# Hybrid two-layer backbone: 512 weight columns per matmul in the products with stationary activations

## The chip, the cores and the metric

The kernel runs on one core of a Trainium2 chip. The metric is device time in microseconds of one execution. The kernel before takes 1544.28 us, the median of 3 runs (1542.03, 1544.28, 1546.81).

## What is computed

There are 256 latent tokens and 256 context tokens of width 2048, and two layers that share their weights between the two sets of tokens. All arithmetic is float32. Cut to what the change touches:

```python
# layer 0 (even): two branches side by side, one output projection
y = concatenate([za * silu(g_a), zb * silu(g_b)], -1) @ w_out      # 512 tokens, [2048, 2048]
# post-norm with a gate: t = ALPHA * x + gate * y; normed, scaled, shifted -> input of layer 1
# layer 1 (odd): grouped-query attention, 16 query heads, 4 key and value heads of 128
q, k, v, g = split(z @ w_in)                # k and v: 512 columns each, for latents and context
q, k = rms_norm(q), rms_norm(k)             # per head; rotary positions on the latents' q and k
o = softmax(q @ [k, k_ctx].T * 128 ** -0.5) @ [v, v_ctx]
y = (o * silu(g)) @ w_out                   # latents only: 256 tokens, [2048, 2048]
# again t = ALPHA * h + gate * y, and a layer norm over the 2048 columns gives the output
```

## The kernel before, in words

**Split products.** Each operand is kept as the sum of a high and a low part of type fp32r, and each product is three matmuls (high times high, high times low, low times high). Activations lie transposed in `big_h` and `big_l` (channels on the partitions, 16 tiles of 128 channels, 512 tokens: context first, then latents).

**The weight stream** (class `Stream`, from line 338). Weights come in pieces of 1024 words a partition (512 KB). A piece is loaded from SyncE's queue, ScalarE makes its high part (`high`: hi<-raw or hix<-raw), VectorE subtracts to get the low part (`low`: lo<-raw,hi or lox<-raw,hi). There are four buffers for raw pieces and four or more for each part; a buffer comes free when its last reader is through. `fill` (line 395) issues high and low parts as far ahead as there are buffers, `get` (line 415) calls `fill` and hands out the next piece. In the last projection `ws.more(wpool3, hi=3, lo=4)` (line 1852) makes the low buffers eight, and the `ws.fill()` behind it issues low parts up to eight pieces ahead at once.

**Two kinds of products.** `aform` has the weights stationary (128 output columns) and moves tokens. `bform` (line 497) has the activations stationary and moves the weights: 256 output columns, two token tiles side by side in the two halves of one PSUM bank. It is made of four `bpart`s (line 506), each of one weight piece of 4 k tiles by 256 columns and 24 matmuls of 128x256: 12 for the first token tile, `pump()`, 12 for the second, `pump()`. The banks of products come from `mbank`, a pool of two used in turn (line 265).

**Order of the work.** The program is unrolled in Python and its order is final: each engine executes what it was given in that order, and the first instruction that has to wait holds up all behind it on its engine. `Clock` and `Timed` estimate where each engine is while the program is written out. Generators that were handed to `background` (norms, key processing, attention heads, adaLN products) get their next step issued by `pump()` once that estimate says its inputs are ready; `force` issues the rest of one of them.

**Layer 0's output projection** (`layer0_half`, line 1566), once for the context, once for the latents: eight chunks of 256 columns. Each is one `bform`, then on VectorE, for both token tiles at once, `t = product * gate` (the read that frees the bank), `t = ALPHA * xp + t`, and two `bn_stats`. `xp` is loaded by GpSimd's queue. The first two context chunks are begun ahead, with the channels of the S5 branch first. `norm_h1` (line 1587) norms the whole half in the background, its 1/std on GpSimd, and turns it into `big_h`, `big_l` over PSUM banks of the pool `bb` (five banks here, line 1543).

**Keys and values of layer 1** (from line 1704), context then latents: four `bform`s, two for keys, two for values. Each of the key ones starts `k_done` (line 1682) in the background: step 1 copies the product (ScalarE `kn`), squares and sums it and computes 1/rms with twelve small GpSimd instructions (`rms`, line 1659); step 2 scales and rotates on VectorE; step 3 transposes on TensorE into a bank of `bb` and splits the result.

**Heads of layer 1** (line 1788): for each pair of heads one `bform` for queries, two `aform`s for gates, and attention in the background with banks of `bb`.

**The last projection** (from line 1808): chunks of 256 columns. Three quarters of each of the first two are begun among the last heads. After their last quarters ScalarE copies both into `t`, then comes `ws.fill()`, and then a loop over chunks 0 to 5: `load_h1(n + 1)` (GpSimd's queue; two buffers), the `bform` of the chunk (for n of 2 and more), `h1(n)` (two VectorE instructions `xp<-xp,gbr` that rebuild the layer's input), `t = product * gate1`, `t = ALPHA * xp + t`, `bn_stats`. The last two chunks run one token tile after the other, so that the norm of the first lies behind the products of the second. The norm's gain and shift `gf` are loaded by GpSimd's queue behind the last `load_h1` (lines 1866 and 1867).

Of the kernel before, what the change touches and what calls it, by code (L numbers as in the profile page):

```python
# [23 lines left out]
F32 = mybir.dt.float32  # L24
# [3 lines left out]
OP = mybir.AluOpType  # L28
# [4 lines left out]
T = 256            # latent tokens, and as many context tokens  # L33
NT = 512           # tokens in all: context first, then latents
# [19 lines left out]
class Clock:  # L54
    """Estimates of when each engine is through with what was issued to it, for the order of issue: engines run
    what they are given in order, an instruction waits for those that wrote what it reads and for those that
    read or wrote what it writes."""
# [72 lines left out]
    def dma(self, q, words, descr, outs, ins):  # L130
# [5 lines left out]
        while left > 0:                                       # room in buckets of 2 us  # L136
# [10 lines left out]
    def slot(self, pool, name, bufs, tile):  # L147
        """The tile takes the place of the one of that name bufs tiles ago."""
# [15 lines left out]
    def free(self, pool, name, bufs, n=1):  # L164
        """When n more tiles of that name have their places free."""
# [17 lines left out]
class Pool:  # L183
    """A pool whose tiles the clock knows."""
# [16 lines left out]
class Timed:  # L201
    """An engine whose instructions advance the clock."""
# [46 lines left out]
def backbone(ctx: ExitStack, tc: tile.TileContext, A, out):  # L249
# [15 lines left out]
    mm = pool(ctx, name="mm", bufs=2, space=bass.MemoryType.PSUM)  # L265
# [17 lines left out]
    def vacant():  # L283
        """Steps until the bank of hbank() is free."""
# [7 lines left out]
    def mbank():  # L292
        return mm.tile([P, 512], F32, name="m")
# [4 lines left out]
    # ---------------------------------------------------------------- constants  # L298
# [5 lines left out]
    negm = tabs[:, 0:64]                                     # window of the neighbourhood  # L304
# [3 lines left out]
    # small vectors as columns: 0 c, 16 c_ctx, 32 ln_g0, 48 ln_b0, 64 glu_b  # L308
# [11 lines left out]
    # silu of both conditioning vectors as stationary columns (32 wide, the rest zero)  # L320
# [10 lines left out]
    # sums over two sets of the vectors' shifts and scales  # L331
# [3 lines left out]
    mod = [const.tile([P, 2, 2, KT], F32, name=f"mod{l}") for l in range(2)]   # [shift|1+scale, c|c_ctx, kt], from the biases on  # L335

    # ---------------------------------------------------------------- streamed weights
    class Stream:
        """Pieces of weights, each at most PIECE words a partition, loaded and split ahead of their use."""
# [3 lines left out]
        def __init__(self):  # L343
# [3 lines left out]
            self.cap = CAP                            # pieces loaded ahead of use, at most  # L347
# [7 lines left out]
        def tile(self, kind, dtype):  # L355
            """In place of the oldest of its kind."""
# [38 lines left out]
        def fill(self):  # L395
            """Low and high parts as far ahead as there is room, and loads."""
# [13 lines left out]
        def ahead(self):  # L410
            """Loads, once there is room for them."""
# [3 lines left out]
        def get(self):  # L415
            """The next piece; those behind it are on their way."""
# [9 lines left out]
    # ---------------------------------------------------------------- background work  # L426
    bg = []                                                   # [generator, when its next step may be issued]
# [5 lines left out]
    def force(b, done=lambda: False):  # L433
        """Issue the steps of one of them up to a point that what follows builds on."""
# [1513 lines left out]
```

## Time and profile before

| what | us |
|---|---|
| median of the runs | 1544.28 |
| span of the profiled execution (the page gives no other time of it) | 1544.0 |
| TensorE busy | 1489.3 (96%) |
| VectorE busy | 983.3 (64%) |
| ScalarE busy | 642.2 (42%) |
| GpSimd busy | 153.5 (10%) |
| chain that ended last | TensorE 80%, VectorE 6%, DMA 5%, issue 4% |

A matmul's recorded duration is longer than its distance to the next one, because matmuls are pipelined; how fast TensorE works is read from the distances of their starts. A row of a timeline is: start, duration, engine, line, operation, output<-inputs, shapes, how many in a row are merged, and in brackets the idle time before it and what ended it. All instructions have the line of one helper (L212), so tiles tell them apart: `m<-hi,big_h` is a product of the weight stream, `b<-ident,...` a transpose.

### The profile page before, as it was taken

To read this page: it belongs to the slowest core of one execution; us is meant where nothing else is said; L and a number is where in the kernel's file an instruction comes from. 1 tells how busy PE (TensorE), PEld (TensorE's weight loads), DVE (VectorE), ACT (ScalarE), POOL (GpSimd) and SP (SyncE) were. 2 spreads that over 40 slices of the span, in tenths; PEclk is the share of its full clock that TensorE was granted. 3 is DMA by queue.
4 is the path that set the end of the run, shared out by engine and by line. 5 is a ranking of instruction groups with operands and counts; after the bars stand their busy time and mean duration, and the time that the engine had idled before them with its cause. 6 is when DMAs were issued, how large, how long until landed. Compare 5 with 4: busy or idle time off the path is not lost.

```text
span 1544.0 us, 30572 instructions
## 1 busy us (share of the span) xinstructions
PE 1489.3 (96%) x12530; PEld 1276.8 (83%) x12530; DVE 983.3 (64%) x1721; ACT 642.2 (42%) x981; POOL 153.5 (10%) x308
## 2 busy tenths in 40 slices
PE   6999988999999999999999999999999999999995
PEld 3676776677699977888887899999998888999995
DVE  5356489988522787545476564866764555677587
ACT  2332334422355434434353433543543445665540
POOL 1000000000000032300000000201321111121021
PEclk9999999999999999999999999999999999999998
DMA  9999365676888686543479998665658775445684
GB/s 327 338 320 305 115 187 185 202 238 219 256 294 260 175 201 153 150 142 110 128 229 316 308 314 259 190 196 167 219 183 269 246 232 178 137 124 151 204 255 141
DMA packets 329921, 332.71 MB, mean 215 GB/s; under 512 B 40197, under 2 KB 287925, under 8 KB 329141
## 3 DMA queue, kind: packets, MB, share of 16 engines
q1 hardware_dynamic: 323540, 314.87, 65.6%
q0 software_dynamic: 6240, 15.88, 3.9%
q8 instruction: 98, 1.61, 0.4%
q14 instruction: 43, 0.34, 0.1%
HBM read 301.92 MB, written 24.54 MB: 211 GB/s over the span
## 4 chain that ended last, share of the span: by engine, by line
PE 80%; DVE 6%; DMA 5%; issue 4%; POOL 2%; SPq 1%; ACT 1%; DVEq 0%; POOLq 0%; ACTq 0%
PE m L212 60%; PE b L212 10%; PE a L212 6%; PE sb L212 4%; DVE dd L212 2%; SPq L212 1%; DVE t L212 1%; DMA aw<-in_ada_w_dram 1%; DMA gf<-in_ln_b_dram 1%; DMA nat<-in_s_c_im_dram 1%; DVE lo L212 1%; DMA adp<-in_ada_w_dram 1%; POOL gbr L212 1%; POOL rt L212 1%; DMA xs<-in_x_dram 0%
## 5 line engine op out<-in xcount | busy, mean ns | idle before, releaser
L212 ACT ACTIVATE hi<-raw 128x1024 fp32r<-128x1024 f32 (+1 forms) x253 | 265.3, 1050 | 313.6 <-PE m L212 170.8
L212 PE MATMUL m<-hi,big_h 128*128 128x256 f32 x1224 | 352.9, 288 | 1.4 <-DVE t L212 1.4
L212 PE MATMUL m<-hi,big_l 128*128 128x256 f32 x1224 | 346.2, 283 | 0.0
L212 DVE TENSOR_TENSOR lo<-raw,hi 128x1024 fp32r<-128x1024 f32 (+1 forms) x214 | 257.3, 1209 | 110.4 <-issue 56.3
L212 PE MATMUL m<-lo,big_h 128*128 128x256 f32 x1152 | 325.7, 283 | 0.0
L212 PE MATMUL m<-big_h,hi 128*128 128x512 f32 (+1 forms) x848 | 321.4, 379 | 2.1 <-DVE acc L212 1.4
L212 PE MATMUL m<-big_l,hi 128*128 128x512 f32 (+1 forms) x848 | 309.0, 364 | 0.0
L212 PE MATMUL m<-big_h,lo 128*128 128x512 f32 (+1 forms) x832 | 304.4, 366 | 0.0
L212 PEld LDWEIGHTS m<-hi,big_h 128*128 128x128 f32 x1224 | 234.2, 191 | 17.3 <-issue 16.2
L212 PEld LDWEIGHTS m<-hi,big_l 128*128 128x128 f32 x1224 | 234.3, 191 | 0.2 <-DVE big_l L212 0.2
L212 PEld LDWEIGHTS m<-lo,big_h 128*128 128x128 f32 x1152 | 220.7, 192 | 0.2
L212 PEld LDWEIGHTS m<-big_h,hi 128*128 128x128 f32 x848 | 159.9, 189 | 47.7 <-issue 20.0
L212 PEld LDWEIGHTS m<-big_h,lo 128*128 128x128 f32 x832 | 156.9, 189 | 26.6
L212 PEld LDWEIGHTS m<-big_l,hi 128*128 128x128 f32 x848 | 160.3, 189 | 20.7
L212 PE MATMUL m<-lox,big_h 128*128 128x256 f32 x384 | 108.6, 283 | 0.0
L212 PE MATMUL m<-hix,big_h 128*128 128x256 f32 x312 | 89.3, 286 | 0.0
L212 PE MATMUL m<-hix,big_l 128*128 128x256 f32 x312 | 88.2, 283 | 0.0
L212 POOL DMA_DIRECT2D Yd<-ys x64 | 37.7, 595 | 409.3 <-DVE ys L212 408.6
L212 PE MATMUL a<-aw,cst 128*32 128x256 f32 x1024 | 75.6, 388 | 2.1 <-DMA aw<-in_ada_w_dram 2.1
L212 PEld LDWEIGHTS m<-lox,big_h 128*128 128x128 f32 x384 | 73.6, 192 | 0.2
L212 ACT ACTIVATE hix<-raw 128x1024 fp32r<-128x1024 f32 x45 | 47.5, 1056 | 58.9 <-PE m L212 26.0
L212 DVE TENSOR_TENSOR lox<-raw,hi 128x1024 fp32r<-128x1024 f32 x39 | 47.7, 1222 | 25.7 <-PE m L212 11.9
(383 smaller groups left out, 2184.5 us busy)
## 6 DMA issues: line engine op xcount, KB each, us to landing
aw<-in_ada_w_dram SPq DMA_DIRECT2D x128, 512.0 KB, 5.2
raw<-in_od_w_in_dram SPq DMA_DIRECT2D x96, 512.0 KB, 3.6
raw<-in_ev_w_in_dram SPq DMA_DIRECT2D x90, 512.0 KB, 5.4
adp<-in_ada_w_dram SPq DMA_DIRECT2D x64, 512.0 KB, 7.3
raw<-in_ev_w_out_dram SPq DMA_DIRECT2D x64, 512.0 KB, 5.6
raw<-in_od_w_out_dram SPq DMA_DIRECT2D x32, 512.0 KB, 3.4
ub<-Ud SPq DMA_DIRECT2D x32, 128.0 KB, 6.2
Sd<-sx SPq DMA_DIRECT2D x16, 256.0 KB, 7.2
```

The costliest lines, as they stand in the source:

```text
L212: r = f(*a, **kw)
```

## The change

The products with stationary activations of layer 0's output projection, of layer 1's keys and values, and of the last projection take 512 weight columns at a time: `wide` in place of `bform`, each token tile in a bank of its own. A weight piece is now 2 k tiles by 512 columns, and a `wide` takes eight. The queries' `bform` stays as it was. The pool of products' banks has a third bank from layer 0's output projection on, and `bb` has four instead of five. `k_done` now works on one token tile of four heads, not on two heads of two token tiles. Core of the diff (definitions of weights' order and comments left out):

```diff
+    mring = [(mm, "m0"), (mm, "m1")]
     def mbank():
+        mring.append(mring.pop(0))
+        p, name = mring[-1]
+        return p.tile([P, 512], F32, name=name)
...
+    def wpart(ps, t, t0, korder, a):
+        wh, wl = wide_w
+        c = t0 + t * P
+        for k in range(2):
+            kk = korder[a * 2 + k]
+            PE.matmul(ps, big_h[:, kk, c:c + P], wh[:, k, :], start=a == 0 and k == 0, stop=False)
+            PE.matmul(ps, big_h[:, kk, c:c + P], wl[:, k, :], start=False, stop=False)
+            PE.matmul(ps, big_l[:, kk, c:c + P], wh[:, k, :], start=False, stop=a == 7 and k == 1)
+        pump()
+    def wide(t0, done, korder=tuple(range(KT)), ps=None, a0=0):
+        ps = ps or [mbank(), mbank()]
+        for a in range(a0, 8):
+            wide_w[:] = ws.get()
+            for t in range(2):
+                wpart(ps[t], t, t0, korder, a)
+                if a == 7:
+                    done(t, ps[t])
...
-    bb = pool(ctx, name="bb2", bufs=5, space=bass.MemoryType.PSUM)
+    bb = pool(ctx, name="bb2", bufs=4, space=bass.MemoryType.PSUM)
+    mring.insert(0, (pool(ctx, name="mm2", bufs=1, space=bass.MemoryType.PSUM), "m2"))
...  layer0_half
-        for n in range(8):
+        for n in range(4):
+            def done(i, ps):
+                V.tensor_mul(t[:, i, cs], ps, gate[:, v, cs])
+                V.scalar_tensor_tensor(t[:, i, cs], xp[:, i], ALPHA, t[:, i, cs], op0=OP.mult, op1=OP.add)
+                V.bn_stats(st_[:, i, n], t[:, i, cs])
+            if hf == 0 and n == 0:
+                wide(0, done, OUT_ORDER, ps0, 4)
             else:
-                ps = bform(hf * T, OUT_ORDER)
+                wide(hf * T, done, OUT_ORDER)
...  keys and values
+        def keys(t, ps):
+            kb_.append(background(k_done(hf, t, ps)))
+            pump()
+        def values(t, ps):
+            act(vh[:, 2 * hf + t], ps)
+            V.tensor_sub(vl[:, 2 * hf + t], ps, vh[:, 2 * hf + t])
+        wide(hf * T, keys)
+        wide(hf * T, values)
...  last projection (six pieces of chunk 0 are begun among the last heads)
+        load_h1(0)
+        load_h1(1)
+        def columns(n, i, ps):
+            if i == 0:
+                inputs(n)                         # xps[2n], xps[2n + 1] = h1(2n), h1(2n + 1)
+            cs = slice(n * 512, n * 512 + 512)
+            V.tensor_mul(t[:, i, cs], ps, gate1[:, cs])
+            for c in range(2):
+                o = t[:, i, n * 512 + c * 256:n * 512 + c * 256 + 256]
+                V.scalar_tensor_tensor(o, xps[2 * n + c][:, i], ALPHA, o, op0=OP.mult, op1=OP.add)
+            V.bn_stats(st_[:, i, n], t[:, i, cs])
+        wide(0, lambda i, ps: act(t[:, i, :512], ps), range(KT), first_ps, NX)
         ws.more(wpool3, hi=3, lo=4)
         ws.fill()
+        for n in range(3):
+            if n > 0:
+                wide(0, lambda i, ps: columns(n, i, ps))
+            else:
+                for i in range(2):
+                    columns(0, i, t[:, i, :512])
+            for c in (2 * n + 2, 2 * n + 3):
+                load_h1(c)
         GP.dma_start(gf[:, 0], dram(A["ln_g"], D, [[0, P], [1, D]]))
         GP.dma_start(gf[:, 1], dram(A["ln_b"], D, [[0, P], [1, D]]))
```

Behind that, the last 512 columns of the first token tile are one product of 48 matmuls, those of the second token tile two products of 256 columns each, as before.

## Rows read from the trace of the kernel before

**Rows 1.** Stretches: length; PE, PEld, DVE, ACT, POOL busy; PEclk; DMA; GB/s.

```profile
845.00:960.00 115.00, 115.00 (x960) 100.29 (x959) 66.56 (x83) 43.57 (x48) 6.47 (x9) 1.00 0.91 302
960.00:1062.00 102.00, 102.00 (x855) 102.00 (x854) 70.43 (x97) 43.72 (x50) 10.86 (x19) 1.00 0.62 193
1062.00:1110.00 48.00, 45.32 (x377) 44.75 (x376) 34.39 (x56) 22.44 (x30) 21.61 (x44) 1.00 0.63 202
1420.00:1500.00 80.00, 78.58 (x644) 77.61 (x643) 56.69 (x77) 37.41 (x50) 12.91 (x24) 1.00 0.75 218
```

**Rows 2.** Waits of PE, 845 to 1544: us in total, times, longest.

```profile
PE b L212 <- DVE t L212: 2.7, 2, 1.8
PE m L212 <- DVE t L212: 1.4, 1, 1.4
PE b L212 <- DVE kf L212: 0.9, 2, 0.7
```

**Rows 3.** Chain that ended last: start, us, what (unbroken runs of matmuls).

```profile
193.08 15.21 PE m L212 x66
...
795.89 10.89 PE m L212 x48
...
1007.33 53.29 PE m L212 x444
```

**Rows 4.** Timeline of DVE, layer 0's output projection.

```profile
883.81 0.69 DVE L212 TENSOR_TENSOR t<-m,gate 128x512 f32<-128x512 f32 x1 [6.84 <-DMA gate<-Ad]
```

**Rows 5.** Timeline of ACT, first key product of the latents.

```profile
1125.88 0.60 ACT L212 ACTIVATE kn<-m 128x512 f32<-128x512 f32 x1 [1.82 <-PE m L212]
```

**Rows 6.** Timeline of POOL, its 1/rms (the first and the last of 12).

```profile
1128.57 1.10 POOL L212 TENSOR_TENSOR rt<-rr 128x4 f32<-128x4 f32 x1 [26.12 <-DVE rr L212]
...
1134.34 0.20 POOL L212 TENSOR_TENSOR rr<-rr,rt 128x4 f32<-128x4 f32 x1
```

**Rows 7.** Timeline of DVE, the same keys.

```profile
1134.57 0.69 DVE L212 TENSOR_TENSOR kn<-kn,rr 128x512 f32<-128x512 f32 x1 [1.77 <-POOL rr L212]
```

**Rows 8.** Timeline of PE, the same keys.

```profile
1137.52 0.66 PE L212 MATMUL b<-ident,kf 128*128 128x128 f32 x4 [0.15 <-DVE kf L212]
```

**Rows 9.** Timeline of PE, last projection, chunks 3 and 4.

```profile
1480.43 0.28 PE L212 MATMUL m<-hix,big_l 128*128 128x256 f32 x1
1482.13 0.36 PE L212 MATMUL m<-hi,big_h 128*128 128x256 f32 x1 [1.42 <-DVE t L212]
```

**Rows 10.** Timeline of DVE, last projection, chunks 0 to 2.

```profile
1468.55 1.23 DVE L212 TENSOR_TENSOR lo<-raw,hix 128x1024 fp32r<-128x1024 f32 x1 [0.20 <-ACT hix L212]
1469.69 1.41 DVE L212 TENSOR_TENSOR xp<-xp,gbr 128x512 f32<-128x512 f32 x2
...
1476.57 2.34 DVE L212 TENSOR_TENSOR lo<-raw,hi 128x1024 fp32r<-128x1024 f32 x2
...
1479.97 1.41 DVE L212 TENSOR_TENSOR xp<-xp,gbr 128x512 f32<-128x512 f32 x2
1481.30 0.68 DVE L212 TENSOR_TENSOR t<-m,gate 128x512 f32<-128x512 f32 x1
```

**Rows 11.** Timeline of ACT, last projection: high parts of late pieces.

```profile
1482.68 1.06 ACT L212 ACTIVATE hix<-raw 128x1024 fp32r<-128x1024 f32 x1 [7.14 <-DMA raw<-in_od_w_out_dram]
...
1487.31 1.06 ACT L212 ACTIVATE hix<-raw 128x1024 fp32r<-128x1024 f32 x1 [0.34 <-DMA raw<-in_od_w_out_dram]
```

**Rows 12.** Stretches behind 3.5 us without matmuls (columns as in Rows 1).

```profile
592.00:593.00 1.00, 0.35 (x6) 0.35 (x8) 0.99 (x3) 0.00 (x0) 0.00 (x0) 0.58 1.14 318
598.00:599.00 1.00, 1.00 (x6) 0.90 (x6) 0.82 (x2) 0.00 (x0) 0.00 (x0) 0.51 0.70 121
```

**Rows 13.** Timeline of PE, its last matmul.

```profile
1528.15 0.28 PE L212 MATMUL m<-hix,big_l 128*128 128x256 f32 x1
```

**Rows 14.** Timeline of DVE, the end.

```profile
1524.64 0.75 DVE L212 SCALAR_TENSOR_TENSOR t<-t,rs,gf 128x512 f32<-128x512 f32 x1 [0.41 <-DMA gf<-in_ln_b_dram]
...
1528.62 0.42 DVE L212 TENSOR_TENSOR t<-m,gate 128x256 f32<-128x256 f32 x1
```

More of the change, by code (lines that the diff above doesn't have):

```diff
@@ L582, in backbone @@
     for half in range(2):
-        for n in range(0, 8, 2):
-            for n_, ko in ((0, 1), (1, 1), (0, 0), (1, 0)) if n == 0 and half == 0 else ((0, 1), (0, 0), (1, 1), (1, 0)):
-                ws.add(W_OUT, D, ko * 8, 8, (n + n_) * 256, 256)
+        for n in range(4):
+            for ko in (1, 0):
+                ws.add(W_OUT, D, ko * 8, 8, n * 512, 512)
     for half in range(2):
-        for n in range(4):
-            for ko in (0, 1):
-                ws.add(X_IN, OD_IN, ko * 8, 8, 2048 + n * 256, 256)
+        for n in range(2):
+            ws.add(X_IN, OD_IN, 0, KT, 2048 + n * 512, 512)
     for hp in range(8):
@@ L1533, in backbone @@
     OUT_ORDER = tuple(range(8, 16)) + tuple(range(8))
-    ps0 = [mbank().rearrange("p (t n) -> p t n", t=2) for _ in range(2)]
+    ps0 = [mbank(), mbank()]
     for i in range(4):
@@ L1537, in backbone @@
             zab = background(za_split())
-        bpart(ps0[i // 2], 0, OUT_ORDER, i % 2)
+        wide_w[:] = ws.get()
+        for t in range(2):
+            wpart(ps0[t], t, 0, OUT_ORDER, i)
     force(zab)
@@ L1838, in backbone @@
         NH = 2
-        for n in range(NH - 1):
-            load_h1(n)
+        load_h1(0)
+        load_h1(1)
         def h1(n):
@@ L1852, in backbone, with inputs @@
+        xps = {}
+        def inputs(n):
+            for c in (2 * n, 2 * n + 1):
+                xps[c] = h1(c)
+        wide(0, lambda i, ps: act(t[:, i, :512], ps), range(KT), first_ps, NX)
         ws.more(wpool3, hi=3, lo=4)
         ws.fill()
-        for n in range(N1):
-            cs = slice(n * 256, n * 256 + 256)
-            load_h1(n + 1)
-            ps = t[:, :, cs] if n < NX else bform(0)
-            xp = h1(n)
-            V.tensor_mul(t[:, :, cs], ps, gate1[:, None, cs].to_broadcast([P, 2, 256]))
-            V.scalar_tensor_tensor(t[:, :, cs], xp, ALPHA, t[:, :, cs], op0=OP.mult, op1=OP.add)
-            for i in range(2):
-                V.bn_stats(st_[:, i, n], t[:, i, cs])
@@ L1886, in backbone @@
-            V.bn_aggr(mv[:, i], st_[:, i])
+            for c in range(1 + i):
+                w = slice(256 * c, 256 * c + 512 - 256 * i)
+                ps = mbank()[:, w]
+                for a in range(8):
+                    if i == 0:
+                        pieces.append(ws.get())
+                    for k in range(2):
+                        wh, wl = (x[:, k, w] for x in pieces[a])
+                        xh, xl = (x[:, 2 * a + k, i * P:(i + 1) * P] for x in (big_h, big_l))
+                        PE.matmul(ps, xh, wh, start=a == 0 and k == 0, stop=False)
+                        PE.matmul(ps, xh, wl, start=False, stop=False)
+                        PE.matmul(ps, xl, wh, start=False, stop=a == 7 and k == 1)
+                if i == 0:
+                    columns(3, i, ps)
+                else:
+                    o = t[:, i, 1536 + 256 * c:1536 + 256 * c + 256]
+                    V.tensor_mul(o, ps, gate1[:, 1536 + 256 * c:1536 + 256 * c + 256])
+                    V.scalar_tensor_tensor(o, xps[6 + c][:, i], ALPHA, o, op0=OP.mult, op1=OP.add)
+                    V.bn_stats(st_[:, i, 3 + c], o)
@@ L1887, in backbone @@
+            V.bn_aggr(mv[:, i], st_[:, i, :4 + i])
             rs2 = inv_std(mv[:, i:i + 1], 1)
```

110 lines of the change are left out of this document (38 added, 72 removed).

## The prediction, made before the changed kernel was run

> **What bounds the kernel now.** I read the page first: TensorE is busy in 96% of the span and has most of the chain that ended last. Then the stretches [rows 1], because the share is a mean: in the two stretches of layer 0's output projection TensorE is busy throughout at a granted clock of 1.00, in the keys and values and in the last projection it has holes of a few us. The waits say what the holes are [rows 2]: 2.7 us for the norm of the latents, 0.9 us for keys that VectorE had not finished, 1.4 us for a bank that VectorE had not read. So wherever the change puts its wider matmuls, TensorE's own pace is the bound, and the three other things are chains through VectorE, GpSimd and loads which just about keep up. The reader is to see two things in this: the pace is worth something over the whole length, and each of these chains has little slack to lose.
>
> **Pace, the gain.** An unbroken run of 444 matmuls of 256 columns takes 53.29 us, 120.0 ns each [rows 3], so 240.0 ns for 512 columns. Runs of 512-column matmuls take 15.21 / 66 = 230.5 ns and 10.89 / 48 = 226.9 ns [rows 3]. In these the weights are stationary and the tokens move; the changed products do it the other way round with the same shapes, so I take the middle, 228.7 ns: 11.3 ns gained for each pair that becomes one. Pairs, from the code: layer 0's projection 2 halves x 4 chunks x 96 = 768; keys and values 2 x 2 x 96 = 384; last projection 3 x 96 + 48 = 336 (the second token tile's last 512 columns stay at 256). 1488 x 11.3 ns = 16.8 us; by the two ends 14.1 and 19.5 us. TensorE has no cover here, so all of it would show. Bytes loaded are the same, in rows of 2 KB rather than 1 KB.
>
> The Trainium skill ("TensorE: Matmul & The Clock Gate", section "Back-to-back issue gap") gives an isolated gap of columns / 2.4 plus 2.5 ns. By that, 256 columns are 109.2 ns and a pair joined saves 2.5 ns, 3.7 us in all. The rows disagree with it at 256 columns by 10.8 ns, and I go by them; what would follow if joining saved nothing is a rival below.
>
> **VectorE's work per chunk.** Gate, residual and statistics work on the same elements with instructions of the same or double width: nothing on the path. High and low parts: as many pieces as before.
>
> **Banks.** Before, a chunk's bank was needed again a whole `bform` later (96 x 120.0 ns = 11.5 us). Now with three banks in turn a `wide` takes the free one for its first token tile and, for its second, the bank of the first token tile of the `wide` before. That is needed again 12 matmuls after its product is complete: 2.7 us. In layer 0 a read of a bank takes 0.69 us [rows 4] and is issued at once, so it fits, except in the first chunk, whose read waits for the gate until 883.81 [rows 4]; there the bank is read at 884.5, about when it is wanted. I take 0.3 us (0 to 2). `bb` loses a bank: a pair of heads takes eleven banks in turn, and with four of them each still falls on one that its own inputs have already emptied: 0.
>
> **Keys.** Before, the two `k_done` of a set of tokens started 11.5 us apart; now both start at the end of one `wide`, 6 matmuls (1.4 us) apart. Before, one took: product copied at 1125.88 [rows 5], GpSimd from 1128.57 to 1134.54 [rows 6], scaling from 1134.57 [rows 7], transposes at 1137.52, for which TensorE waited 0.15 us [rows 8]: already just in time, and the transposes stand at the same number of matmuls behind, which now take 0.5 us less. The second `k_done` has to wait for GpSimd's 6.0 us of the first. Its keys are ready some 4 to 6 us after the first ones, while the planner, which knows GpSimd as faster than it is, puts its transposes perhaps 4 us behind. TensorE then waits 2 to 2.5 us for context and for latents alike, 4.3 us, less the 0.9 us of before [rows 2]: 3.4 us (0 to 7). The wait for the norm of the latents (2.7 us) comes a fixed time after layer 0's last product while TensorE is 0.7 us faster through what lies between: 0.7 us more. Together 4.1 us (0 to 7.7). VectorE stands still while it waits for GpSimd, and low parts queue behind it; four pieces are ready ahead, 11 us, which covers that.
>
> **Last projection.** Here the chain matters most. Before, chunk 2 began 192 x 120.0 ns before 1480.55 [rows 9], at 1457.5, and TensorE wanted chunk 2's bank again at 1480.55; VectorE read it from 1481.30 to 1481.98 [rows 10], and the next matmul started at 1482.13 [rows 9]: 1.6 us lost. Why so late: VectorE makes the eight pieces of `fill`, held up by loads, until 1469.69; chunks 0 and 1 until 1476.57; three more low parts; one `h1` of 1.33 us (1479.97 to 1481.30); then the read [rows 10].
> Now TensorE begins the second `wide` at the same 1457.5, ends it 96 x 228.7 ns = 22.0 us later, and wants its first bank after 6 more matmuls, at 1480.8. VectorE: 1469.7, plus the 512 columns of the first chunk (6.9 us for the same elements, and two more instructions: 7.3), plus seven low parts, because eight pieces are fetched by then instead of four (2.34 / 2 each [rows 10]: 8.2), plus two `h1` (2.7), plus the read (0.7): 1488.6. TensorE is then held for 7.8 us instead of 1.6: 6.2 us lost. That is the lower end. The upper: the fifth of these low parts needs a raw buffer that the first gives back; before, the piece so loaded reached ScalarE at 1482.68, 6.1 us after the low parts began at 1476.57, and the second piece behind it at 1487.31 [rows 11]. The same steps from 1477.0 end at 1493.4: 11.0 us lost. I take 7.5, nearer to the lower, as 2 KB rows can only help the loads.
> What is queued behind VectorE's late read: the rest of that chunk, then `load_h1` for the third, which still come 15 us ahead of their use.
>
> **Clock.** After 3.5 us without matmuls the granted clock was 0.58 and then about 0.5 (the 1.2 GHz level) from 592.6 to 599.0 [rows 12]: 6.4 us at half speed cost 3.2 us. The 1.6 us and 2.7 us of the waits above left it at 1.00 [rows 1]. A hold of over 7 us will cost something: 2.0 us (0 to 3.2).
>
> **End.** TensorE's last matmul starts at 1528.15 [rows 13], and VectorE, which had waited for `gf` until 1524.64, comes to the second token tile at 1528.62 [rows 14]. In the changed kernel `gf` is asked for some 20 us before TensorE's end, behind four more loads; by my times VectorE again comes to it as TensorE ends. 0 (-1.3, what waiting for `gf` cost, to +4).
>
> **Sum.** -16.8 + 0.3 + 4.1 + 7.5 + 2.0 + 0 = -2.9 us. The profiled execution's span is 1544.0, the median 1544.28, so it is a typical one, and I put the sum on the median: 1541.4 us.
>
> **Rivals.**
> (1) VectorE comes in time. If 2 KB rows let the loads behind `fill` land some 4 us sooner, VectorE's whole chain moves up by that, the hold shrinks to about 2 us more than before with the clock intact, and GpSimd, undisturbed by a standing VectorE, halves the wait for keys. For it: `fill` is held up by loads, not by work (0.20 us before its last low part was still a wait [rows 10]). Against it: 15.5 us of plain VectorE work follow anyway. -16.8 + 0.3 + 2 + 2 = -12.5: 1531.8 us.
> (2) Slower, by VectorE's read of the second chunk's first bank in the last projection: loads at the upper end (11.0), the full price of the clock (3.2), and `gf`, which stands behind loads that wait for the same late chunks, late by 4: -16.8 + 0.3 + 4.1 + 18.2 = +5.8: 1550.1 us. It decides from where hold, clock and end together cost 12.4 us. For it: the late high parts [rows 11]. Against it: DMA is busy for only 0.75 of that stretch [rows 1].
> (3) Joining two matmuls saves nothing with stationary activations: then the gain is 0 and the losses stay, +13.9: 1558.2 us. Against it: both runs of 512 columns [rows 3]. It is the direction in which the skill's formula points, which leaves 3.7 us of the gain and would end at 1554.5.
> (4) The wide products start where they should but TensorE waits so often for banks that the pace is lost everywhere: 1544, no change.
>
> **How the numbers follow.** Forecast 0.50 (its own range 1537 to 1546), rival (1) 0.26, (2) 0.16, (3) 0.04, (4) 0.04. A change of 0.3% (4.6 us, about what a measurement of this kernel can tell from none) lies at 1539.6 and 1548.9. The forecast's range gives 0.17 to faster and 0.33 to no change, (1) 0.26 to faster, (2) 0.13 to slower and 0.03 to no change, (3) slower, (4) no change: faster 0.43, same 0.40, slower 0.17. The range 1531 to 1551 leaves out half of (1)'s lower side, some of (2) and all of (3).
>
> **What would show it.** Pace: distances of 128x512 starts in `m<-hi,big_h` near 229 ns (wrong at 240). Last projection: one hole of TensorE ended by VectorE's `t`, 6 matmuls into the third `wide`, of about 9 us, and a lower granted clock behind it. Keys: waits for `kf`, longer for the second token tile. Layer 0: none over 1 us. The prediction is wrong if there is no such hole, or if holes turn up at every `wide`.

## The result, and the profile after

The changed kernel is slower. Its median is 1554.55 us over four runs (1553.90 to 1556.06), that of the kernel before 1544.97 us over four runs; the ratio is 1.006 (95% interval 1.0044 to 1.0075). Run once more later, beside other kernels, it came out at 1.0037 (1.0020 to 1.0053), so totals of different groups of runs that differ by less than some 4 us show nothing by themselves. The prediction, 1541.4 us in a range up to 1551, had the wrong sign.

The profiled execution after has a span of 1553.4 us, 9.4 us longer than before. Four landmarks that both traces have divide it: ScalarE's last copy of the gated unit's output (`big_h<-gth`, 861.84 after, 859.88 before), the first transpose of the norm of the latents, the second of ScalarE's two copies `t<-m` at the start of the last projection (it ends the first 512 columns in both kernels), and TensorE's last matmul.

| stretch | before | after | difference | predicted |
|---|---|---|---|---|
| up to the gated unit's end (same code) | 859.9 | 861.8 | +2.0 | 0 |
| A: to the norm of the latents (layer 0's projection, first keys) | 216.9 | 214.9 | -1.9 | -9.0 |
| B: to the copy (other keys, values, heads) | 381.0 | 376.2 | -4.8 | -0.6 |
| C: to TensorE's last matmul (last projection) | 70.4 | 81.5 | +11.0 | about +7 |
| D: to the end of the span | 15.8 | 19.0 | +3.1 | 0 |

The predicted column is the prediction's sum laid on these stretches, by the wide products that the trace after has in each: 825 of the 1488 in A, 415 in B, 240 in C. The first row is the spread of code that wasn't touched: in the seventeen profiled runs of this study it ends anywhere from 857.4 to 865.3.

The chain that ended last, after (start, us, what), has the pace:

```profile
950.23 16.36 PE m L212 x72
...
1016.30 42.23 PE m L212 x186
```

That is 227.2 and 227.0 ns for 512 columns, against 240.0 ns for two matmuls of 256 [rows 3]. The waits of TensorE after, 845 to 1554 (us in total, times, longest), against those of before [rows 2]:

```profile
PE m L212 <- DVE t L212: 15.3, 2, 12.9
PE b L212 <- DVE t L212: 3.1, 3, 1.5
PE a L212 <- DMA aw<-in_ada_w_dram: 1.9, 2, 1.0
PE b L212 <- DVE kf L212: 0.5, 1, 0.5
PE m L212 <- DVE lo L212: 0.2, 1, 0.2
```

One line is new in size, 15.3 us for banks that VectorE had not read. The timeline of PE has its two holes, at the place the prediction named and at one it priced at 0.3:

```profile
890.55 0.79 PE L212 MATMUL m<-hi,big_h 128*128 128x512 f32 x1 [2.40 <-DVE t L212]
...
1475.63 0.39 PE L212 MATMUL m<-hi,big_l 128*128 128x512 f32 x1
1488.89 0.79 PE L212 MATMUL m<-hi,big_h 128*128 128x512 f32 x1 [12.87 <-DVE t L212]
```

What VectorE did ahead of the second of these reads (timeline of DVE):

```profile
1464.45 2.74 DVE L212 TENSOR_TENSOR xp<-xp,gbr 128x512 f32<-128x512 f32 x4
...
1471.35 2.34 DVE L212 TENSOR_TENSOR lo<-raw,hi 128x1024 fp32r<-128x1024 f32 x2
1473.61 2.36 DVE L212 TENSOR_TENSOR lox<-raw,hi 128x1024 fp32r<-128x1024 f32 x2
1480.51 1.22 DVE L212 TENSOR_TENSOR lox<-raw,hix 128x1024 fp32r<-128x1024 f32 x1 [4.55 <-ACT hix L212]
1483.01 2.57 DVE L212 TENSOR_TENSOR lox<-raw,hix 128x1024 fp32r<-128x1024 f32 x2 [1.27 <-ACT hix L212]
1485.49 2.74 DVE L212 TENSOR_TENSOR xp<-xp,gbr 128x512 f32<-128x512 f32 x4
1488.15 0.69 DVE L212 TENSOR_TENSOR t<-m,gate 128x512 f32<-128x512 f32 x1
```

The reader is to see one queue: the first chunk's column work (1464.45 to 1471.35), four low parts, three more that wait 4.55 and 1.27 us for loads, the inputs of the second chunk, and only then the read that TensorE has wanted since 1476.0. The load behind the first wait, on ScalarE:

```profile
1479.42 1.06 ACT L212 ACTIVATE hix<-raw 128x1024 fp32r<-128x1024 f32 x1 [6.49 <-DMA raw<-in_od_w_out_dram]
```

And what SyncE's queue, which issues the loads, waited for from 1455 to 1485 (us in total, times, longest): low parts, which give its buffers back. The 7.6 us fit the first chunk's column work, which stands ahead of the low part at 1471.35.

```profile
SPq L212 <- DVE lox L212: 11.4, 7, 2.5
SPq L212 <- DVE lo L212: 9.1, 3, 7.6
```

Ahead of the first hole's read, in layer 0, stand low parts of the same kind (DVE again); the profile puts ScalarE's wait behind them down to TensorE here, and to the weight load in e1 below (9.40 us):

```profile
886.61 1.23 DVE L212 TENSOR_TENSOR lo<-raw,hi 128x1024 fp32r<-128x1024 f32 x1 [7.02 <-ACT hi L212]
...
889.81 0.68 DVE L212 TENSOR_TENSOR t<-m,gate 128x512 f32<-128x512 f32 x1
```

The stretches after (columns as in [rows 1]; the last two are the ones behind the two holes):

```profile
845.00:960.00 115.00, 111.67 (x591) 78.24 (x590) 63.27 (x72) 42.21 (x48) 3.62 (x5) 0.99 0.87 300
960.00:1062.00 102.00, 101.22 (x463) 83.47 (x462) 73.05 (x93) 45.58 (x52) 7.82 (x15) 1.00 0.61 200
1420.00:1500.00 80.00, 67.13 (x317) 55.98 (x317) 52.00 (x70) 36.31 (x48) 10.88 (x18) 0.91 0.68 210
890.00:895.00 5.00, 4.45 (x17) 2.69 (x18) 4.86 (x7) 3.17 (x3) 0.71 (x1) 0.66 0.73 270
1490.00:1495.00 5.00, 5.00 (x14) 3.88 (x13) 4.66 (x7) 1.06 (x1) 3.30 (x6) 0.53 0.30 78
```

Behind the long hole thirteen products start 0.43 us apart, the 1.2 GHz level, until 1494.6; at 0.2275 us they would have taken 2.7 us less. Hold and half speed together are 15.6 us, all that stretch C has beyond its bare products (240 at 0.2275 and 96 at 0.120 us are 66.1 us, 15.4 below 81.5). The end, on PE and on DVE [rows 13, 14]:

```profile
1534.41 0.28 PE L212 MATMUL m<-hix,big_l 128*128 128x256 f32 x1
```

```profile
1522.44 0.69 DVE L212 TENSOR_TENSOR xp<-xp,gbr 128x512 f32<-128x512 f32 x1 [2.48 <-DMA gbr<-in_ln_g_dram]
...
1527.40 0.69 DVE L212 TENSOR_TENSOR xp<-xp,gbr 128x512 f32<-128x512 f32 x1 [1.86 <-DMA gbr<-in_ln_b_dram]
...
1538.05 0.42 DVE L212 TENSOR_TENSOR t<-m,gate 128x256 f32<-128x256 f32 x1
```

VectorE waits for the last inputs' gains and shifts, which GpSimd requested only between 1518.07 and 1522, behind the third chunk's column work, and comes to the second token tile 3.6 us after TensorE's last matmul, not 0.5.

### The profile page after: what moved, and what is told of

The parts are those of the page before. It is cut to its first block, busy times and chain, and to the rows that moved or that the text cites. A ratio compares the mean times of both kernels' runs of the same rounds, so it can differ in the third digit from the quotient of the medians.

```text
span 1553.4 us, 27566 instructions
## 1 busy us (share of the span) xinstructions
PE 1478.6 (95%) x11042; PEld 1198.6 (77%) x11042; DVE 981.7 (63%) x1699; ACT 642.5 (41%) x981; POOL 147.1 (9%) x300
## 4 chain that ended last, share of the span: by engine, by line
PE 72%; DVE 9%; DMA 8%; issue 6%; POOL 3%; SPq 1%; ACT 1%; DVEq 0%; POOLq 0%; ACTq 0%
PE m L212 53%; PE b L212 9%; PE a L212 6%; PE sb L212 4%; DVE dd L212 2%; DMA aw<-in_ada_w_dram 2%; SPq L212 1%; DVE t L212 1%; DMA raw<-in_ev_w_out_dram 1%; DVE lo L212 1%; POOL rt L212 1%; DMA nat<-in_s_b_im_dram 1%; DMA raw<-in_ev_w_in_dram 1%; DMA nat<-in_s_c_im_dram 1%; DMA adp<-in_ada_w_dram 1%
## 5 line engine op out<-in xcount | busy, mean ns | idle before, releaser
L212 PE MATMUL m<-hi,big_h 128*128 128x256 f32 (+1 forms) x848 | 289.3, 341 | 15.3 <-DVE t L212 15.3
L212 PE MATMUL m<-hi,big_l 128*128 128x256 f32 (+1 forms) x848 | 282.0, 333 | 0.0
L212 PE MATMUL m<-lo,big_h 128*128 128x256 f32 (+1 forms) x806 | 266.9, 331 | 0.2 <-DVE lo L212 0.2
L212 PEld LDWEIGHTS m<-hi,big_h 128*128 128x128 f32 x848 | 162.1, 191 | 44.2 <-DVE t L212 16.1
L212 PEld LDWEIGHTS m<-hi,big_l 128*128 128x128 f32 x848 | 162.2, 191 | 15.8
L212 PEld LDWEIGHTS m<-lo,big_h 128*128 128x128 f32 x806 | 154.4, 192 | 13.5 <-DVE lo L212 0.6
L212 PE MATMUL m<-lox,big_h 128*128 128x512 f32 (+1 forms) x234 | 82.3, 352 | 0.0
L212 PE MATMUL m<-hix,big_h 128*128 128x512 f32 (+1 forms) x192 | 68.2, 355 | 0.0
L212 PE MATMUL m<-hix,big_l 128*128 128x512 f32 (+1 forms) x192 | 67.1, 349 | 0.0
L212 PEld LDWEIGHTS a<-aw,cst 128*32 128x32 f32 x1024 | 23.2, 108 | 35.5 <-issue 18.1
```

The costliest lines, as they stand in the source:

```text
L212: r = f(*a, **kw)
```

## The experiments

There are fifteen runs, one of them (e9) the changed kernel again, each beside the kernel before. The edits are abridged. A to D are the stretches of the table above. The theories took shape on the way: T, the last projection's hold carries the loss, because VectorE reads the bank late (rival L: another part of the change does; R-A: only the inputs ahead of the read; R-C: the loads are late anyway); T2, the low parts of a whole chunk stand ahead of that read; T3, VectorE's blocks of column work hold up the low parts, and with them the load buffers.

| run | ratio to before (95%) | A | B | C | D |
|---|---|---|---|---|---|
| e1_last_as_before | 0.9954 (0.9938 to 0.9970) | 216.5 | 376.5 | 68.8 | 15.4 |
| e2_last_alone | 1.0085 (1.0068 to 1.0103) | 217.0 | 381.0 | 83.7 | 18.7 |
| e3_read_first | 1.0024 (1.0009 to 1.0039) | 213.2 | 374.3 | 81.2 | 17.6 |
| e4_third_other_banks | 1.0019 (1.0004 to 1.0034) | 216.9 | 374.2 | 78.9 | 20.4 |
| e5_four_ahead | 1.0025 (1.0010 to 1.0040) | 213.9 | 374.8 | 82.2 | 15.2 |
| e6_three_repairs | 0.9937 (0.9918 to 0.9956) | 210.3 | 376.8 | 74.7 | 14.4 |
| e7_l0_banks | 0.9924 (0.9904 to 0.9944) | 211.2 | 377.3 | 68.8 | 16.7 |
| e8_tail | 1.0013 (0.9998 to 1.0027) | 216.4 | 374.9 | 78.9 | 15.6 |
| e9_after_again | 1.0037 (1.0020 to 1.0053) | 214.0 | 374.9 | 83.1 | 19.0 |
| e10_four_raw | 1.0002 (0.9985 to 1.0019) | 214.3 | 374.9 | 73.0 | 26.1 |
| e11_eight_raw | 0.9980 (0.9966 to 0.9995) | 213.9 | 375.5 | 70.8 | 23.8 |
| e12_all | 0.9930 (0.9910 to 0.9951) | 211.0 | 375.6 | 75.5 | 15.7 |
| e13_first_later | 1.0046 (1.0029 to 1.0063) | 215.2 | 375.0 | 83.3 | 20.1 |
| e14_first_later_8raw | 0.9976 (0.9955 to 0.9997) | 213.3 | 374.4 | 69.3 | 23.8 |
| e15_best | 0.9896 (0.9876 to 0.9916) | 210.2 | 375.7 | 66.9 | 14.4 |

**Which part of the change carries the loss.** e1 is the kernel after with the last projection's weights, its begun chunks and its last stage as before; e2 the kernel before with these three as after.

```
e1: -    NX = 6;  ws.add(X_OUT, D, 0, KT, n * 512, 512)     first_ps, last stage: wide(...)
    +    NX = 2;  ws.add(X_OUT, D, a * 4, 4, n * 256, 256)  first_ps, last stage: bpart, bform
e2: the same lines the other way round, in the kernel before, with the three banks in turn
```

> Half of the change: layer 0's output projection and the key and value passes stay in chunks of 512, the last projection is put back to 256 columns in half a bank. Theory T (the loss sits in the last projection, where TensorE stood 12.87 us for the bank of the second chunk's first tile and ended 3.1 us earlier against the span's end than before): the trace after was 4.6 us ahead at the end of the chunk begun ahead of the last heads, of which this kernel keeps what layer 0 and the passes gained (3 to 5), and the last projection takes what it took before, so 1539 to 1543, a ratio to before of 0.996 to 0.999. Rival L (layer 0's hold of 2.40 us and its slower weight loads, or the passes, carry the loss): 1550 or more, a ratio above 1.003.

> The other half alone: the kernel before with only the last projection in chunks of 512 (with its three product banks). Theory T: the hold of 12 to 13 us at the third chunk and the later end are all here, so the kernel is slower by what the last projection lost in the trace after, 11 to 14 us: 1555 to 1558, a ratio of 1.007 to 1.009, and a row of some 13 us for TensorE waiting on VectorE in the last projection. Rival L: within 3 us of before, ratio 0.998 to 1.002. Together with the kernel that keeps the other half the two differences should add to the +9.6 us measured for the whole change.

e1 is 7 us faster than before, more than expected, and e2 13 us slower. In e2's timeline of PE:

```profile
1494.34 0.79 PE L212 MATMUL m<-hi,big_h 128*128 128x512 f32 x1 [14.91 <-DVE t L212]
```

So the loss is in the last projection, and the layer 0 and key and value parts pay. By their ratios the two add up to +6 us; the whole change measured +9.3 and, run again, +5.7.

**Order within VectorE's column work.**

```
 def columns(n, i, ps):
-    if i == 0: inputs(n)
     V.tensor_mul(t[:, i, cs], ps, gate1[:, cs])
+    if i == 0: inputs(n)
```

> The changed kernel with one order turned round: VectorE reads the finished bank (product by the gate) before it takes the two 256-column inputs of the layer, instead of after. Theory T (the read stands behind the low parts of four pieces that wait for their loads until about 1483, and the two inputs are only 2.7 us of the wait): the hold falls from 12.9 to about 10 us, the total by 2 to 4 to 1551 to 1553. Rival R-A (the place of the inputs ahead of the read makes the hold): the hold falls below 4 us and the total to 1542 or less.

```profile
1486.04 0.80 PE L212 MATMUL m<-hi,big_h 128*128 128x512 f32 x1 [12.38 <-DVE t L212]
```

The hold stays at 12.38 us and C at 81.2. Rival R-A falls, and T's 2.7 us are missing too: counted from the copy, the low part that waits for its load started 2.4 us later than in after (30.0 us, 1450.33 to 1480.36, against 27.6), which ate what the turned order saves. That delay isn't the edit's: the low parts behind the stage's first loads came 10.4 us after the copy in e3, 7.8 in after and 9.3 in the run again. The total is 5.6 us under the first measurement of after, and 2.0 under the second, whose interval overlaps its own: nothing gained is shown.

**Take the bank away.**

```
-    wide(0, lambda i, ps: columns(n, i, ps))
+    wide(0, lambda i, ps: columns(n, i, ps), range(KT), [bank(), bank()] if n == 2 else None)
```

> The changed kernel with the last projection's third chunk in two banks of the ring that the heads used and that stands empty then, so that no product of it waits for a bank that VectorE has still to read; nothing else changes. Theory T, in its form that the bank is what TensorE lacks: no row for TensorE waiting on VectorE's read in the last projection, the half-speed stretch after it (granted clock 0.53 in 1490 to 1495) gone too, 1540 to 1545. In its form that the low parts themselves come late (rival R-C: the weights of the next chunk aren't there either, loads and low parts are the bound): the wait only changes its name, from the bank to the low part of a piece or to its load, of 8 us or more, and the total stays at 1550 or more.

The hold is gone and other waits stand in its place (timeline of PE):

```profile
1498.39 0.50 PE L212 MATMUL b<-lo,big_h 128*128 128x512 f32 x1 [0.90 <-DVE lo L212]
1506.49 0.50 PE L212 MATMUL m<-hi,big_h 128*128 128x512 f32 x1 [1.23 <-ACT hi L212]
1507.75 0.50 PE L212 MATMUL m<-lox,big_h 128*128 128x512 f32 x1 [0.76 <-DVE lox L212]
1510.78 0.80 PE L212 MATMUL m<-lox,big_h 128*128 128x512 f32 x1 [0.47 <-DVE lox L212]
1521.27 0.50 PE L212 MATMUL m<-lo,big_h 128*128 128x512 f32 x1 [3.96 <-DVE lo L212]
```

They are 7.3 us in all, the granted clock falls to 0.50 between them (1510 to 1515), and C is 78.9. The wait changed its name, as R-C expected, and came out a little under its 8 us. So the bank was what TensorE waited for, and not what made it late: the weights weren't there either.

**Fewer pieces ahead, so that less stands in front of the read; and three repairs at once.**

```
+    ws.look = 4     # in fill: min(self.n[kind], self.look) pieces ahead
     ws.fill()
```

> The changed kernel with one number changed: in the last projection the low and high parts are made four pieces ahead instead of eight until its last chunk begins (buffers, banks and loads as they are). The trace after has the low parts of pieces 16 to 23 ahead of the read of the second chunk's first bank in VectorE's order, and those of 20 to 23 wait for loads until 1484.7; with four ahead only 16 to 19 stand before it, which were done at 1475.9. Theory T2 (the place of the read behind the low parts of a whole chunk makes the hold): the read comes at about 1478.5, the hold falls from 12.9 to 1 to 4 us and the half-speed stretch goes, 12 to 14 us less than after: a ratio to before of 0.997 to 0.999. Rival R-C (the loads are late whatever the order): the hold goes but TensorE waits 6 us or more for low or high parts, as the 7.3 us in the run with other banks, and the ratio stays at 1.002 or more.

> Three repairs of the changed kernel together: four pieces ahead in the last projection; layer 0's second chunk in two banks of the other ring, so that nothing of it waits for a read; the gains and shifts of the next inputs requested as soon as the last ones are used, ahead of the inputs themselves. T2: the sum of the three, 12 to 14 (hold and half speed) + 3 to 5 (layer 0's hold of 2.4 us and half speed after it) + 2 to 3 (the end, 18.7 us after TensorE's last matmul, back to about 16): a ratio to before of 0.991 to 0.996. R-C: above 1.000.

The waits of PE in e5, from 1400 on:

```profile
PE m L212 <- DVE lox L212: 6.9, 2, 3.7
PE m L212 <- DVE t L212: 2.4, 1, 2.4
PE m L212 <- DVE lo L212: 0.8, 1, 0.8
PE m L212 <- ACT hix L212: 0.7, 1, 0.7
```

The hold is 2.4 us, as T2 said, and C doesn't fall: 82.2. T2's price was wrong. With four ahead the first chunk's column work moved in front of low parts, and VectorE waited in it for the inputs (4.37 and 2.56 us), while DMA was busy for 0.06 of 1460 to 1465: the loads waited for their four buffers, which only a low part gives back. SyncE's queue from 1455 to 1470:

```profile
SPq L212 <- DVE lox L212: 16.1, 3, 14.7
```

e6 came out within T2's range for the sum, but its C, 74.7, is still 8.6 us above the bare products: a right total for a price that e5 shows to be wrong.

**Layer 0 and the end by themselves.**

```
e7 (on e1): - wide(hf * T, done, OUT_ORDER)
            + wide(hf * T, done, OUT_ORDER, [bank(), bank()] if (hf, n) == (0, 1) else None)
e8 (on after): load_h1 in two: load_gbr for the next two inputs right after inputs(n), load_xp where it was
```

> Layer 0 by itself: the kernel with the last projection as before, and in it layer 0's second chunk in two banks of the other ring; nothing else. If layer 0's wait for the read (4.01 us in the run without this) and the half speed after it cost what they show, the total falls by 3 to 6 us below that run's 0.9954 of before, to 0.991 to 0.994. If the read only hides a later wait (the weight loads beside the two gate loads are late), the wait changes its name in the trace and the ratio stays at 0.995 to 0.996.

> The end by itself: the changed kernel, with the gains and shifts of the next two inputs requested right after the last ones are used and ahead of the inputs, so that they no longer stand behind the whole of VectorE's columns; nothing else. If the late requests (POOL 1518 to 1522) make the end longer, the time from TensorE's last matmul to the span's end falls from 18.7 to about 16 us and the total by 2 to 3 us, a ratio of 1.004; the hold stays near 12 us. If the end is long for another reason, it stays at 18 to 19 and the ratio at 1.006.

In e1 layer 0's hole is this row of PE; e7 has no such wait, A falls from 216.5 to 211.2 and the ratio from 0.9954 to 0.9924:

```profile
888.85 0.79 PE L212 MATMUL m<-hi,big_h 128*128 128x512 f32 x1 [4.01 <-DVE t L212]
```

In e8 D falls from 19.0 to 15.6 with the hold still at 11.3 us: the late requests make the long end. Its ratio, 1.0013, is 3.7 us under that of the kernel after run again, but the two intervals overlap; it is the trace that shows it.

**The load buffers.** e9 is the changed kernel again. e10 and e11 differ in one number:

```
e10 (on e4): - ws.more(wpool3, hi=3, lo=4)   + ws.more(wpool3, hi=1, lo=2); the last chunk by wide(...)
e11 (on e10):                                + ws.more(wpool3, raw=4, hi=1, lo=2)
```

> The changed kernel once more, unchanged, beside the three others of this group, as the mark that they are compared with. Every theory expects what was measured first: ratio 1.006 (1.0044 to 1.0075), a hold of 11 to 13 us in the last projection, 81 us from the end of the begun chunk's copy to TensorE's last matmul. If it comes out at 1.003 or less, some 4 us of what the earlier single edits seemed to gain belong to the spread between groups of runs and not to the edits.

> A control for the next run: the kernel with the third chunk in other banks, and the last chunk computed like the others (both token tiles for each piece, so that its pieces need not be kept), which lets the low and high parts be six ahead; loads still go into four buffers. Theory T3 (a load waits for one of four buffers, which VectorE frees by making the low part, and VectorE's block of 7 us of column work, with its own waits, stands ahead of it): TensorE still waits for weights in the last projection, 5 us or more with the half speed behind it, 74 to 80 us from the copy of the begun chunk to the last matmul. The end is longer than before, since the norm of the first tile is no longer behind products. Rival (it was the eight kept pieces or the bank, not the loads): 66 to 70 us already here.

> The control with one thing more: eight buffers for the loads in the last projection instead of four. T3: the loads no longer wait for VectorE, TensorE's waits for weights go, 66 to 69 us from the copy of the begun chunk to the last matmul (65.5 are the bare 288 products of 512 at 0.2275 us), 6 us or more below the control. Rival R-C in its plain form (the DMA engines can't deliver, whatever the buffers): the same waits as in the control, within 2 us.

```profile
1471.22 0.80 PE L212 MATMUL m<-lo,big_h 128*128 128x512 f32 x1 [3.52 <-DVE lo L212]
...
1492.41 0.50 PE L212 MATMUL b<-lo,big_h 128*128 128x512 f32 x1 [0.34 <-DVE lo L212]
...
1516.31 0.50 PE L212 MATMUL m<-lox,big_h 128*128 128x512 f32 x1 [1.84 <-DVE lox L212]
```

```profile
1470.64 0.80 PE L212 MATMUL m<-lo,big_h 128*128 128x512 f32 x1 [2.85 <-DVE lo L212]
```

e9 came out between the two marks of its expectation, with a hold of 14.56 us and 83.1 in C. The first fence is PE in e10, the second in e11, where it is the only wait left in the stage: from 1475 on TensorE is busy throughout and all weights have landed by 1500. But 2.1 us in C is a third of what T3 expected, and hardly more than R-C allowed: the control had already got down to 73.0, below its own 74 to 80. What tells the two apart are the waits, and the 2.85 us stand behind the first chunk's column work.

**The order on VectorE.** e12 is e6 with the first fill eight ahead and the read first.

```
e12 (on e6): ws.fill() ahead of ws.look = 4; inputs(n) after the read
e13 (on after): wide(..., mid=first) for the second chunk: columns(0, ...) after its fourth piece
e14: the same move on e11
e15 (on e12): ws.look = 5; columns(0, ...) after the second chunk's fourth piece;
              inputs(2) after the third chunk's fourth piece
```

> The three repairs with the order put right: the first chunk's columns stay behind eight pieces (there the inputs' loads were what VectorE waited for), the later chunks look four pieces ahead, and the bank is read before the inputs are taken. T3: no wait of VectorE in front of the low parts, a hold under 1 us, 66 to 71 us from the copy to the last matmul against 74.7 in the three repairs, a ratio of 0.988 to 0.992. If the loads are late for a reason other than VectorE's order, the 74 to 75 us stay and the ratio too, at 0.993 to 0.995.

> The changed kernel with one thing moved: the column work of the first chunk (7 us of VectorE; its products are already copied out of the banks, so nothing waits for it) stands in the middle of the second chunk instead of ahead of it. Buffers, banks, the eight pieces ahead and the order in the later chunks as they are. Theory T3: the low parts of pieces 16 to 19 then come some 6 us earlier, with them the loads of 20 to 22 that wait for their buffers, and the read of the second chunk's first bank; the hold falls from 12.9 (14.6 in the run again) to 4 to 8 us and the 81 to 83 us from the copy to the last matmul to 73 to 78, the total to a ratio of 0.999 to 1.002. Rival R-C (the loads are late because the DMA engines are full at the start of the stage: gate, inputs and weights together): the loads land when they did, the hold stays at 11 us or more.

> The same move in the kernel with eight load buffers, other banks for the third chunk and the last chunk computed like the others. There one wait was left, 2.85 us for a low part that stood behind the first chunk's column work, with a half-speed stretch behind it. T3: no wait of TensorE above 1 us is left in the last projection and the granted clock stays at 1.00, 66 to 68 us from the copy to the last matmul (70.8 without the move, 65.5 bare). R-C: the same wait at the same piece, now for its load, 70 us or more.

> What T3 says a kernel with these chunks should be, within the buffers there are: layer 0's second chunk in other banks, gains and shifts requested early, the bank read ahead of the inputs, five pieces ahead, the first chunk's column work in the middle of the second chunk and the inputs of the third in its own middle, so that VectorE never has 7 us of column work in one block. T3: 66 to 71 us from the copy to the last matmul (75.5 in the kernel with the order put right only), a ratio of 0.985 to 0.990, below the 0.9924 of the kernel that leaves the last projection as before. If four load buffers are too few whatever the order, it stays at 73 us or more and 0.991 to 0.994.

e12 missed (75.5): its hold was 1.35 us, but a low part behind the third chunk's 7 us of column work came 2.41 us late, two more waits of 0.99 and 0.77 us followed, and the granted clock fell behind them. e13 missed as well (timeline of DVE):

```profile
1474.34 2.74 DVE L212 TENSOR_TENSOR xp<-xp,gbr 128x512 f32<-128x512 f32 x4
...
1482.36 3.49 DVE L212 TENSOR_TENSOR lox<-raw,hix 128x1024 fp32r<-128x1024 f32 x3
...
1489.64 0.69 DVE L212 TENSOR_TENSOR xp<-xp,gbr 128x512 f32<-128x512 f32 x1 [2.10 <-DMA gbr<-in_ln_g_dram]
...
1491.54 0.68 DVE L212 TENSOR_TENSOR t<-m,gate 128x512 f32<-128x512 f32 x1
```

The loads did come earlier: the last three low parts of the lookahead no longer wait. But the column work now ended only at 1481.2, just ahead of them, and the second chunk's inputs, requested behind it, made VectorE wait 3.1 us more. The hold was 15.11 us: the number that R-C gave, without its reason, since VectorE waited for no weights there. In e14 one wait of 2.52 us remained, for a low part behind the second chunk's inputs (3.4 us of waiting for their loads) and column work, and C was 69.3, not 66 to 68.

e15 holds. The waits of PE, 845 on, and two stretches of it:

```profile
PE b L212 <- DVE t L212: 3.1, 3, 1.5
PE b L212 <- DVE kf L212: 1.7, 2, 1.3
PE m L212 <- DVE t L212: 0.9, 1, 0.9
PE a L212 <- DMA aw<-in_ada_w_dram: 0.6, 2, 0.4
```

```profile
1450.00:1455.00 5.00, 5.00 (x24) 4.14 (x23) 0.60 (x1) 0.00 (x0) 0.00 (x0) 1.00 1.01 350
...
1490.00:1495.00 5.00, 5.00 (x24) 4.14 (x23) 4.83 (x9) 1.15 (x2) 0.22 (x1) 1.00 0.93 314
```

C is 66.9 against 66.1 bare, the clock is 1.00 from 845 to TensorE's last matmul, and the kernel takes 1530.2 us, 16 us (0.9896) less than before: the best of all. In the last projection it has the three banks in turn and the four load buffers of the kernel after, and DMA is as full at the start of the stage (1.01 in 1450 to 1455) as there (1.02 in 1455 to 1460). One part of its edit did nothing: with five pieces ahead the first chunk's column work still stands right behind the low part of piece 15 (1459.76), where e12 has it. What differs from e12 in effect is one more piece ahead of the read and the 2.7 us of inputs taken out of the third chunk's block; the last chunk's inputs also stand ahead of its read again.

**What this settles.** The last projection was lost on VectorE's one queue. It makes the low parts that TensorE needs, frees the load buffers by them, and frees the banks; with 512 columns its column work comes in blocks of 7 us, and whatever stands behind a block or behind a wait inside it is late. Each single edit changed which of the three TensorE saw. Neither the number of banks nor full DMA engines decided by themselves: e15 has both as after in this stage. Not separated is which of e15's two effective steps gave how much of the 8.7 us over e12 in C (each C is of one profiled execution, and in e15 the low parts behind the stage's first loads came 8.5 us after the copy, in e12 10.0), and whether rows of 2 KB land later than rows of 1 KB (512 KB loads of the stage took 5.7 us to land after, 3.5 before, but after they were requested in bursts of four).

## Why the prediction was wrong, by its steps

- **Pace: right, at its upper end.** 13.0 ns a pair [rows 3 and the chain above] where 11.3 were taken, so 19.3 us of gain. B shows its share: 415 pairs are 5.4 us, and B is 5.8 shorter on average over the 13 runs that have all of them wide. A's 825 are 10.7 us, and once its hole is mended A is only 6.2 shorter (210.7 on average in e6, e7, e12 and e15). In e15, where it is 6.7, the starts of the matmuls show the rest: 1.3 us because five and a half more pairs stand ahead of A's end, 1.7 us in short waits and where adaLN products and transposes break into the wide products (7.9 us over the bare pace, 6.2 before), and 1.0 us in the norms' transposes (3.8 us, 2.8 before).
- **Banks in layer 0: wrong, 0.3 taken with 2 as the bound.** The gate [rows 4] was not what held VectorE. Low parts that waited for weight loads stood ahead of the read, which came at 889.81 and not at 883.8; the hold was 2.4 us (1.9 to 4.2 in the runs without e7's repair), then came half speed, together 5 us in A (e1 against e7).
- **Keys: wrong the other way.** 4.1 us taken, nothing lost in waits: TensorE waited 0.5 us for keys where it had waited 0.9, and 2.4 for the norm against 2.7. GpSimd did take 5.7 us for the second token tile after the first, but its transposes came 5.2 us behind the first ones, with 0.5 us of waiting in that.
- **The hold in the last projection: the step that failed.** "I take 7.5, nearer to the lower, as 2 KB rows can only help the loads." The prediction's upper end, with the low parts waiting for loads, had the read done 35.9 us after the second chunk's start (1457.5 to 1493.4), its lower end 31.1 (1488.6); it was done at 1488.8, 36.1 us after that chunk's start at 1452.74. The low parts' two waits, 4.55 and 1.27 us, account for the distance from the lower end. The cost over before was 12.87 - 1.6 = 11.3 us (13.0 in the run again, 13.3 in e2), the upper end and beyond. The formula was right, and the choice between its ends was wrong: the raw buffers' chain [rows 11] was in plain sight and belonged into the sum, since the low parts that waited stood in front of the read. The reason given for the lower end failed too: loads took 5.7 us to land, not less than the 3.5 of before.
- **Clock: right in size behind the hold**, 2.7 us for 2.0. Not in the sum: half speed also stood for 3.4 us behind layer 0's hole and for 3.4 us behind the two waits for the norm (1.49 and 0.86 us), 1.7 us each. The second needs no wide keys: e2 has it with keys of 256 columns, e1 and e15 don't have it.
- **End: wrong, +3.1 for 0.** `gf` was in time; the last inputs' gains and shifts were late, for the reason that rival (2) gave for `gf`. e8 shows it.
- **Rivals.** Rival (2) is what happened, hold, clock and end together, though what came late at the end was not `gf`. Its +5.8 us compares with 9.4 between the profiled spans: the keys that it charged (4.1) and layer 0's hole that it lacked (some 4) nearly cancel, and 2.0 of the other 3.6 lie in code that wasn't touched. Rival (1), loads sooner, is refuted by the 5.7 us that they took. Rivals (3) and (4), pace not gained or lost everywhere, are refuted by the 227 ns. The Trainium skill's formula for an isolated gap ("TensorE: Matmul & The Clock Gate", section "Back-to-back issue gap") makes 512 columns an estimated 215.8 ns. The rows above have 227: 11 ns more, as at 256 columns, so that joining gains 13.0 ns here and not the formula's 2.5.

## What to carry to other kernels

When instructions are joined, ask what the work of the other engines does to its size of block: here TensorE did gain its pace, but VectorE, which works in order, makes its operands and frees both its banks and the load buffers, had its column work doubled to 7 us at a time. Between two ends of a wait, the one to take is that of the slowest link already visible in the trace. And a wait that vanishes with an edit proves nothing until the stage is shorter: e4 removed the hold, e5 all but 2.4 us of it, and both kept most of the loss.

## What the runs showed of the hardware

- Short waits can cost the clock. Behind holes of 2.40 us (layer 0, after), 2.41 us (e12, 1500.40) and 2.52 us (e14) the granted clock fell to 0.66 to 0.77 over the next 5 us; behind one of 2.41 us in e5 (1483.91) it stayed at 1.00, as it did behind the 1.6 us of before [rows 1]. Behind the two waits for the norm, 1.49 and 0.86 us, it fell to 0.66 from 1078 to 1083 in after; behind 1.76 and 0.93 us at the same place before it stayed at 1.00. The length of a short hole alone doesn't tell.
- After the hold of 12.87 us TensorE ran 5.7 us of unbroken products at half speed, 0.43 us for 512 columns, before the clock came back.
- With stationary activations 512 columns take 227 ns, as in the faster of the two runs with stationary weights [rows 3] (the slower has 230.5): no loss of pace showed from turning the operands round.
